# Attention's stores from SP to ACT, the order of two norms left free, and four embedding products ahead of the summed-weight products

## Chip, cores and metric

The kernel runs on one core of a Trainium2 chip. Times are device microseconds (us) of one execution; a time of the kernel is the median of its runs. The engines are named as in the profile: PE (TensorE, matmuls), DVE (VectorE), ACT (ScalarE), POOL (GpSimd), SP (SyncE, which here only issues DMA transfers). Each engine works through its own queue in order. SP and ACT can both issue transfers.

## What is computed

One layer of a decoder trunk for 1024 prompt tokens and 8 x 4 sample tokens, 1056 together, of width 1024. Cut to what matters:

```python
def _layer(x, p, attn_fn, pool_prev, pos0, ...):
    h = _rms(x, n_mix_pre)
    z = h @ w_in                      # q (8 heads x 64) | k, v (2 heads x 64) | pooling (4 x 128)
    a, k_state, v_state = attn_fn(q, k, v)            # window of 128 keys, a sink per head
    m, pool_state = _pool_mixer(u, pool_prev, pos0, w_pool, pool_scale)
    mix = jnp.concatenate([a, m], axis=-1) @ w_out
    x = x + _rms(mix, n_mix_post)
    f = _rms(x, n_ffn_pre)
    f = (jax.nn.silu(f @ w_gate) * (f @ w_up)) @ w_down
    x = x + _rms(f, n_ffn_post)
    x = x + jax.nn.sigmoid(x @ w_ple_gate) * (p @ w_ple)
    return x, k_state, v_state, pool_state
```

Besides y, the layer returns its states: the last 128 prompt keys and values, the last 15 pooling inputs, and the shifted key, value and pooling buffers of the samples. These states are the seven small stores of attention that the change moves.

## The kernel before

**Tiling.** Activations lie with the channels on 128 partitions and the tokens along the free axis. The 1056 tokens are cut into three groups (g = 0, 1, 2) of 352, so that a product is a chain of 128x128 by 128x352 matmuls into one PSUM bank. All float32 operands are split into a high and a low part (`split`, L164 on ACT for the high part, L165 on DVE for the low one), and a product takes three matmuls for each 128 channels: high x high, high x low, low x high (`gemm`, L126 is the line on which every matmul is recorded).

**Order.** The program is put in order by a scheduler that works on a simulated time: an instruction goes to its engine's queue when what it needs is ready there, and among ready ones the one that is written earlier goes first. The written order is therefore not the order of the queues, except where `tc.keep_in_program_order` pins an instruction behind everything written before it on its engine. `pinned[0]` pins the matmuls; `order(ins)` pins while `ordered[0]` is true; `load` pins on SP. Large working tiles share 28 slots (`act_tile`); a tile waits until a slot is free.

**Stages.** First come the three input norms and the pooling columns of w_in (`u_prod`, `u_evict`). A norm is `rstd_steps`: a matmul against ones sums the squares over the partitions, ACT takes the root (L323), DVE the reciprocal (L324) and its two parts (L326, L327), then `dg1` and `dg2` (L331, L337) write them on a diagonal, and a product spreads the diagonal over the partitions. The squares are added in `sum_halves` (L357, L358, L360), whose first addition is pinned through `order`. Then follow k, v and the four q products with the pooling mixer between them, and after them:

- L618 loads the prompt masks `am`. L628 to L636 transpose v; ACT copies the transposes to `vtok`, `vmix` and `vdec` (L630 to L636).
- L637 and L638 store the last keys and values (`kp_o`, `vp_o`); L603 and L604, earlier, store the pooling states (`pp_o`, `ps_o`).
- L757 to L759 load the cached keys `ckt`, the cached values `cvt` and the sample mask `dmt`.
- `dscores` multiplies the sample queries with the cached keys; L770 adds `dmt` to the scores on DVE, `softmax` follows (L659 to L673: maxima on DVE, exponentials on ACT at L667, scaling on POOL at L673). `scores(b)` does it for a block of 128 prompt queries (L706 and L707 put the two halves of the window together).
- `dturned` transposes the sample weights (L120) and copies them (L781, L782), `dvalues` multiplies with the values. Pieces of the output projection (`filler`) are written between these steps to keep PE at work.
- L863 to L865 store the shifted buffers `ks_o`, `vs_o`, `vn_o`; `kse` is put together for that on POOL.
- Then come the eight blocks of prompt queries, the rest of the fillers, and the loads of x for the residual (L880).

All these transfers are issued from SP before. The FFN fills the time from about 260 us to 1010 us.

**The end.** The last sub-layer multiplies x with w_ple_gate (`ple_out` for group 2, and for groups 0 and 1 a scheme with seven half-size products for four: `ple_first` and `ple_rest`). `ple_rest(a, b)` uses sums of two weight tiles, which `w_sums` makes: four additions on POOL (L1008, in place), then ACT and DVE split the two results (`sh`, `sl`). POOL's first addition has to wait until DVE has split half of the raw tile (`w`). It runs for the pairs (1,0), (3,2), (5,4), (7,6). `ple_end` takes the sigmoid (L1219), multiplies with the embedding product p @ w_ple (L1221), adds x (L1223) and stores a piece of y (L1224). The embedding product is six matmuls (`embed`); `embed_early` computes it ahead and keeps it in a tile, as all of group 0 has it:

```python
    for a in (7, 5, 3, 1):
        ple_first(a)
    finish(list(chains))
    for a, b in PAIRS:
        ple_rest(a, b)
```

Of the kernel before, what the change touches and what calls it, by code (L numbers as in the profile page):

```python
# [19 lines left out]
SEQ = 1024  # L20
NDEC, DSEQ = 8, 4
# [10 lines left out]
WIN = 128  # L32
NB = SEQ // WIN
# [28 lines left out]
def trunk_kernel(  # L62
# [31 lines left out]
    nc = tc.nc  # L94
    te, ve, se, ge = nc.tensor, nc.vector, nc.scalar, nc.gpsimd
# [14 lines left out]
    def act_tile(shape, dt=F32, s="a"):  # L110
        return apool.tile(shape, dt, tag="a", bufs=A_SLOTS, name=nm(s))

    def half(g, dt=F32, s="h"):
        return act_tile([P, 4, NS[g]], dt, s)
# [15 lines left out]
    def bank():  # L130
        return psum.tile([P, 512], F32, tag="b", name=nm("b"))

    def tmp(n, s="t", dt=F32):
        return spool.tile([P, n], dt, tag="tmp", bufs=6, name=nm(s), padded_shape=[P, NX])

    def const(shape, src=None, s="c", dt=F32):
        t = cpool.tile(shape, dt, name=nm(s))
        if src is not None:
            nc.scalar.dma_start(t, src)
        return t  # L140
# [17 lines left out]
    def fix(ins):  # L158

        if fixed[0]:  # L160
            tc.keep_in_program_order(ins)
# [76 lines left out]
    WPE = [[], []]  # L238
# [14 lines left out]
    W1 = {a: WPE[0][a] if a == KC - 1 else None for a, _ in PAIRS}  # L253
# [16 lines left out]
    def need(k, ahead=LOOK):  # L270

        for i in range(len(made), min(k + ahead + 1, len(ITEMS))):
            kind, js = ITEMS[i]
            if kind in ("direct", "home"):
                w_split(js[0], act_tile if kind == "home" else None)
                made[i] = pairs[js[0]]
            elif kind == "half":
                w_load(js[0])
                t = w_tile([P, KC, P], "w2")
                made[i] = t[:, 0:4, :], t[:, 4:8, :]  # L280
                split(*made[i], raws[js[0]][:, 4:8, :])
            else:
                for j in js:
                    w_load(j)
                made[i] = w_sums(*(raws[j] for j in js))
            for kind, js in ITEMS[i + 1 : i + 3]:
                for j in js:
                    w_load(j)
        return made[k]

    def gemm(ps, ops, start=True, stop=True):

        last = len(ops) - 1
        for i, (wh, wl, xh, xl) in enumerate(ops):
            mm(ps, wh, xh, start=start and i == 0, stop=False)
            mm(ps, wh, xl, start=False, stop=False)
            mm(ps, wl, xh, start=False, stop=stop and i == last)
# [9 lines left out]
    ordered = [True]  # L307
# [46 lines left out]
    def sum_halves(sqs, g):  # L354

        a, b = sqs
        order(ve.tensor_tensor(a, a, b, op=ALU.add))  # L357
        ve.tensor_tensor(a[:, 0:2, :], a[:, 0:2, :], a[:, 2:4, :], op=ALU.add)  # L358
        acc = acc_tile(g)
        ve.tensor_tensor(acc, a[:, 0, :], a[:, 1, :], op=ALU.add)  # L360
        return acc
# [37 lines left out]
    def x_squares(g):  # L399
        sqs = [xr[g, h] for h in range(2)]  # L400
        for t in sqs:
            fix(se.activation(t, t, AF.Square))
        acc1[g] = sum_halves(sqs, g)
# [57 lines left out]
    stt, pso = (sts[:, i * n : (i + 1) * n].rearrange("p (c b t) -> p c b t", c=4, t=PST) for i in range(2))  # L461
    pfx = sts[:, 2 * n : 2 * n + 64].rearrange("p (c t) -> p c t", c=4)
    ppo = sts[:, 2 * n + 64 :].rearrange("p (c t) -> p c t", c=4)
# [24 lines left out]
    def u_prod(c, g, h):  # L488

        if h == 0:  # L490
            ups[c, g] = bank()
        ps = ups[c, g][:, : NS[g]]
        wh, wl = pairs[U0[c]]
        xh, xl = xs[g][h]
        for k in range(4):
            mm(ps, wh[:, 4 * h + k, :], xh[:, k, :], start=h == 0 and k == 0, stop=False)
            mm(ps, wh[:, 4 * h + k, :], xl[:, k, :], start=False, stop=False)
        for k in range(4):
            mm(ps, wl[:, 4 * h + k, :], xh[:, k, :], start=False, stop=h == 1 and k == 3)

    def u_evict(c, g):
        for v, cols in toks(us[c], g):
            ve.tensor_tensor(v, like(ups[c, g][:, cols], v), like(r1[g][:, cols], v), op=ALU.mult)

    def u_norm(steps, g):
        try:
            next(steps)
        except StopIteration as e:
            se.copy(acc1[g], e.value)
            r1[g] = acc1[g]  # L510
# [9 lines left out]
    x_operand(2, 0, behind=True)  # L520
    u_norm(norms[0], 0)
    x_squares(1)
    for c in range(4):
        u_evict(c, 0)
        if c:
            u_prod(c, 1, 0)
# [21 lines left out]
    for c in (2, 3):  # L548
        for h in range(2):
            u_prod(c, 2, h)  # L550
        u_evict(c, 2)

    ordered[0] = False

    def u_pool(c):
        ue, dec = us[c], u_decode(c)
# [43 lines left out]
        if 1 <= i < 5:  # L600
            u_mix(i - 1)
    kT, vT, qT = qkv[0], qkv[1], qkv[2:]
    nc.sync.dma_start(pp_o, ppo)  # L603
    nc.sync.dma_start(ps_o, pso)  # L604
    pinned[0] = False


# [1 line left out]
    qd, am, vdec = misc[:, 0, :], misc[:, 1:5, :], misc[: NDEC * DSEQ, 5, :]  # L609
# [5 lines left out]
        own = qm[:, c * n : c * n + NDEC * QS].rearrange("p (b s) -> p b s", s=QS)  # L615
        ge.tensor_copy(own[:, :, :DSEQ], new.rearrange("p (b j) -> p b j", j=DSEQ))
    ys = [[half(g, s="y"), None] for g in range(G)]
    nc.sync.dma_start(am, masks)  # L618
    nskp, nskd = const([P, 8]), const([P, 2])
    ge.tensor_scalar(nskp, skp, -1.0, None, op0=ALU.mult)  # L620
    ge.tensor_scalar(nskd, skd, -1.0, None, op0=ALU.mult)
# [1 line left out]
    vtok, vmix = act_tile([P, NB, P]), act_tile([P, NB, P])  # L623
# [10 lines left out]
    ps = bank()  # L634
    te.transpose(ps[: NDEC * DSEQ, :P], vT[:, SEQ:], ident)
    se.copy(vdec, ps[: NDEC * DSEQ, :P])  # L636
    nc.sync.dma_start(kp_o, kT[:, SEQ - WIN : SEQ])  # L637
    nc.sync.dma_start(vp_o, vtok[:, NB - 1, :])  # L638

    def put(o, lo_tok, n):  # L640

# [112 lines left out]
    cvt = act_tile([P, NDEC, P])  # L754
# [89 lines left out]
    def filler(n):  # L844
        for _ in range(n):
            if fill:
                f, *at = fill.pop(0)
                f(*at)
# [11 lines left out]
    kse = act_tile([P, NDEC, WIN])  # L860
    ge.tensor_copy(kse[:, :, : WIN - DSEQ], ckt[:, :, DSEQ:])
    ge.tensor_copy(kse[:, :, WIN - DSEQ :], kT[:, SEQ:].rearrange("p (b t) -> p b t", t=DSEQ))
    nc.sync.dma_start(ks_o, kse)  # L863
    nc.sync.dma_start(vs_o, cvt[DSEQ:, :, :])
    nc.sync.dma_start(vn_o, vdec)  # L865
    for a, b in zip(blocks, blocks[1:] + [None]):
        t2 = None if b is None else scores(b)
        filler(1)
# [2 lines left out]
        values(a, parts)  # L871
        t = t2
    filler(len(fill))


    x1 = [[None] * 2 for _ in range(G)]
# [15 lines left out]
    def turn(n):  # L892

        now[0] += n
        for ch in [ch for ch in chains if ch[2]] or list(chains):
            while ch in chains and ch[1] <= now[0]:
                try:
                    load, wait = next(ch[0])
                except StopIteration:
                    chains.remove(ch)  # L900
                    break
                dve[0] = max(dve[0], now[0]) + load / share[0]
                ch[1] = dve[0] + wait
# [5 lines left out]
    def finish(ch_list):  # L909
        for ch in ch_list:  # L910
            for _ in ch[0]:
                pass
            chains.remove(ch)
# [107 lines left out]
    def quarter(w, h):  # L1021
        return tuple(t[:, 4 * h : 4 * h + 4, :] for t in w)
# [174 lines left out]
    def embed(wp, m, g):  # L1197

        ph, pl = pls[g]
        wh, wl = need(wp)  # L1200
        cols = slice((m % 4) * P, (m % 4 + 1) * P)
        pp = bank()
        gemm(pp[:, :N], [(wh[:, k, cols], wl[:, k, cols], ph[:, k, :], pl[:, k, :]) for k in range(2)])
        turn(6)
        return pp[:, :N]

    def embed_early(m, g, tiles=[None, None]):

        if m % 4 == 0:
            tiles[m // 4] = half(g, s="pp")  # L1210
        v = tiles[m // 4][:, m % 4, :]
        se.copy(v, embed(WPE[0][m][0], m, g))
        early[m, g] = v

    def ple_end(gate, wp, m, g):

        pp = early.pop((m, g)) if (m, g) in early else embed(wp, m, g)
        sg = tmp(N, "sg")
        se.activation(sg, gate, AF.Sigmoid)  # L1219
        xm = x2[g][m // 4][:, m % 4, :]  # L1220
        ve.tensor_tensor(sg, sg, pp, op=ALU.mult)  # L1221
        yo = tmp(N, "yo")
        ve.tensor_tensor(yo, sg, xm, op=ALU.add)  # L1223
        nc.sync.dma_start(y_o[:, m, OFF[g] : OFF[g + 1]], yo)  # L1224
# [9 lines left out]
    def product(w, x):  # L1234
        ps = bank()
        gemm(ps[:, :N], ops4(w, x))
        turn(12)
        return ps[:, :N]
# [3 lines left out]
    def ple_first(a):  # L1242

        wp, w = W1[a]
        need(wp)
        wg = need(w)
        if not p1s:
            p1s.append(half(0, s="p1"))
        p1 = p1s[0][:, a // 2, :]
        se.copy(p1, product(quarter(wg, 0), e7["B11"]))  # L1250
        c11 = tmp(N, "c11")
        ve.tensor_tensor(c11, p1, product(quarter(wg, 1), e7["B21"]), op=ALU.add)
        ple_end(c11, wp, a, 0)
# [32 lines left out]
        last_down(END, m, 1)  # L1286
    chain(ple_steps(1), 54)
    for m in range(FIRST):
        embed_early(m, 0)
    for m in range(FIRST, KC):  # L1290
        ple_out(m, 2)
        embed_early(m, 0)
    finish(chains[:1])
    for a in (7, 5, 3, 1):
        ple_first(a)
    finish(list(chains))
    for a, b in PAIRS:
        ple_rest(a, b)
# [86 lines left out]
```

## Time and profile before

| | |
|---|---|
| median of 3 runs | 1138.85 us (1133.57 to 1139.66) |
| profiled execution | 1138.72 us |
| span of its instructions | 1136.7 us |
| PE busy | 1111.0 us (98%) |
| DVE / ACT / POOL busy | 783.9 / 457.9 / 201.2 us |
| mean granted TensorE clock | 0.991 |

The profiled execution's own time is 2.0 us longer than its span: the rest lies before the first and behind the last instruction. PE is busy nearly all the time, so what is to be read is the list of places where PE isn't, and what ended each of these gaps. In a row of the timeline stand the start (us from the span's start), the duration (us; a merged row covers several instructions), the engine, the line, the operation, out<-in by tile names, the shapes and the count; in brackets stands how long the engine had been idle before it and what ended that. SPq and ACTq are the queues' DMA issues. In a row of the windows stand the stretch, its length, and for each engine the busy time and the number of instructions, then the granted TensorE clock, the share of the DMA engines' time and GB/s.

### The profile page before, as it was taken

What the parts mean: (1) busy time and instruction counts of PE and PEld (TensorE: products, weight loads), DVE (VectorE), ACT (ScalarE), POOL (GpSimd) and SP (SyncE); (2) the same over time, 40 slices, a digit from 0 to 9 for tenths busy, and PEclk for the clock granted to TensorE, in tenths of its full rate; (3) what the DMA queues carried; (4) which work ended last, traced back from release to release, by engine and by line L of the source; (5) the groups of instructions that cost most, each with busy time, mean ns of one, the idle gap of its engine ahead of it and who ended that gap; (6) DMA issues with size and microseconds to landing.
All of it is one profiled execution on the core that took longest, in us unless ns stands there. A gap on an engine that the chain in (4) does not pass through costs nothing.

```text
span 1136.7 us, 17509 instructions
## 1 busy us (share of the span) xinstructions
PE 1111.0 (98%) x6997; PEld 1091.9 (96%) x6997; DVE 783.9 (69%) x1296; ACT 457.9 (40%) x819; POOL 201.2 (18%) x169
## 2 busy tenths in 40 slices
PE   9999979999999999999999999999999999999987
PEld 8999967899999999999999999999999999999987
DVE  6666268975879955255464555548887877788887
ACT  8322257754646523331222313123524324356442
POOL 1044022200000131011111102111231132100241
PEclk9999989999999999999999999999999999999999
DMA  7121210362553212121110202113212212245241
GB/s 284 56 69 49 86 52 25 121 245 71 194 171 122 101 37 75 38 74 38 37 64 12 81 32 75 37 38 125 79 48 93 75 56 93 94 144 201 76 140 74
DMA packets 35985, 101.78 MB, mean 90 GB/s; under 512 B 4260, under 2 KB 14916, under 8 KB 35904
## 3 DMA queue, kind: packets, MB, share of 16 engines
q1 hardware_dynamic: 35616, 100.62, 26.1%
q8 instruction: 55, 0.90, 0.3%
q14 instruction: 26, 0.21, 0.1%
q10 hardware_dynamic: 288, 0.05, 0.0%
HBM read 90.55 MB, written 10.11 MB: 89 GB/s over the span
## 4 chain that ended last, share of the span: by engine, by line
PE 89%; DVE 5%; POOL 2%; issue 2%; ACT 1%; DMA 1%; POOLq 0%; SPq 0%; DVEq 0%; ACTq 0%
PE b L126 88%; POOL wr L1008 2%; PE b L120 1%; ACT sh L164 0%; DMA wr<-in_w_gu_dram 0%; DVE o L1131 0%; DVE wl L165 0%; DVE sg L1221 0%; DMA a<-in_dmask_dram 0%; DVE yo L1223 0%; ACT a L667 0%; DMA xr<-in_x_dram 0%; ACT wh L164 0%; DVE o L1150 0%; DVE x L1154 0%
## 5 line engine op out<-in xcount | busy, mean ns | idle before, releaser
L126 PE MATMUL b<-hid,wh 128*128 128x352 f32 x1056 | 254.7, 323 | 2.6 <-DVE o L1150 2.2
L164 ACT CAST wh<-wr 128x1024 fp32r<-128x1024 f32 (+1 forms) x135 | 138.6, 1029 | 254.0 <-PE b L126 203.3
L126 PE MATMUL b<-fh,wl 128*128 128x352 f32 x712 | 230.5, 324 | 0.0
L126 PE MATMUL b<-fh,wh 128*128 128x352 f32 x712 | 230.5, 324 | 0.0
L126 PE MATMUL b<-fl,wh 128*128 128x352 f32 x712 | 229.0, 322 | 0.0
L1008 POOL TENSOR_TENSOR wr<-wr 128x512 f32<-128x512 f32 x52 | 72.0, 1385 | 745.9 <-DVE wl L165 460.1
L165 DVE TENSOR_TENSOR wl<-wr,wh 128x1024 fp32r<-128x1024 f32 (+1 forms) x135 | 165.3, 1227 | 44.1 <-ACT wh L164 43.6
L126 PEld LDWEIGHTS b<-hid,wh 128*128 128x128 f32 x1056 | 185.1, 189 | 3.3 <-issue 2.4
L126 PE MATMUL b<-hid,wl 128*128 128x352 f32 x528 | 170.7, 323 | 0.0
L126 PE MATMUL b<-fh,sh 128*128 128x352 f32 x416 | 135.2, 325 | 2.9 <-ACT sh L164 1.9
L1105 DVE TENSOR_TENSOR o<-o,b 128x352 f32<-128x352 f32 x240 | 115.1, 515 | 31.7 <-PE b L126 31.5
L126 PE MATMUL b<-fh,sl 128*128 128x352 f32 x416 | 135.0, 325 | 0.7 <-DVE sl L165 0.7
L126 PEld LDWEIGHTS b<-fl,wh 128*128 128x128 f32 x712 | 135.3, 190 | 0.0
L126 PE MATMUL b<-fl,sh 128*128 128x352 f32 x416 | 134.2, 323 | 0.0
L126 PEld LDWEIGHTS b<-fh,wh 128*128 128x128 f32 x712 | 133.8, 188 | 0.0
L126 PEld LDWEIGHTS b<-fh,wl 128*128 128x128 f32 x712 | 133.7, 188 | 0.0
L165 DVE TENSOR_TENSOR sl<-wr,sh 128x1024 fp32r<-128x1024 f32 x52 | 63.6, 1222 | 81.5 <-ACT sh L164 81.3
L164 ACT CAST sh<-wr 128x1024 fp32r<-128x1024 f32 x52 | 54.0, 1048 | 146.4 <-POOL wr L1008 105.3
L126 PE MATMUL b<-h,wh 128*128 128x352 f32 x480 | 105.7, 326 | 1.3 <-ACT h L392 1.1
L126 PEld LDWEIGHTS b<-hid,wl 128*128 128x128 f32 x528 | 98.9, 187 | 0.0
L126 PEld LDWEIGHTS b<-h,wh 128*128 128x128 f32 x480 | 82.4, 190 | 2.3 <-ACT h L392 1.3
L126 PEld LDWEIGHTS b<-fh,sh 128*128 128x128 f32 x416 | 78.5, 189 | 3.4 <-ACT sh L164 2.2
(186 smaller groups left out, 1693.6 us busy)
## 6 DMA issues: line engine op xcount, KB each, us to landing
wr<-in_w_gu_dram SPq DMA_DIRECT2D x64, 512.0 KB, 3.2
wr<-in_w_dn_dram SPq DMA_DIRECT2D x32, 512.0 KB, 3.5
wr<-in_w_pg_dram SPq DMA_DIRECT2D x18, 512.0 KB, 3.3
x<-in_x_dram SPq DMA_DIRECT2D x6, 704.0 KB, 10.3
x1d<-x SPq DMA_DIRECT2D x6, 704.0 KB, 3.6
x<-x1d SPq DMA_DIRECT2D x6, 704.0 KB, 6.2
out_y_dram<-yo SPq DMA_DIRECT2D x24, 176.0 KB, 1.8
wr<-in_w_out_b_dram SPq DMA_DIRECT2D x8, 512.0 KB, 3.4
```

Source lines behind the costliest of these rows:

```text
L120: ins = te.transpose(out, src, ident)
L126: ins = te.matmul(*args, **kw)
L164: fix(se.copy(hi, src))
L165: fix(ve.tensor_tensor(lo, src, hi.bitcast(F32), op=ALU.subtract))
L1008: ge.tensor_tensor(out, a, b, op=op)
L1105: ve.tensor_tensor(o, o, v, op=ALU.add)
```

## The change

It has three parts.

1. The seven stores of the states (`pp_o`, `ps_o`, `kp_o`, `vp_o`, `ks_o`, `vs_o`, `vn_o`) are taken from SP; they are written behind the last `filler` and issued from ACT. The load of the prompt masks (`am`) is issued from ACT too, at its old place.
2. `ordered[0] = False` stands behind the squares of group 1 rather than behind the whole stage, so that `order` no longer pins the first addition of the squares of group 2 and the diagonals of groups 1 and 2.
3. `embed_early` gets the index of the weights as an argument, and four calls for group 1 (m = 0 to 3) stand between `ple_first` and `ple_rest`. `ple_end` then finds these four products in a tile of group 1 (a new tile of the 28 slots).

```diff
     x_squares(1)
+    ordered[0] = False
     for c in range(4):
         u_evict(c, 0)
...
-    ordered[0] = False
-
...
-    nc.sync.dma_start(pp_o, ppo)
-    nc.sync.dma_start(ps_o, pso)
...
-    nc.sync.dma_start(am, masks)
+    nc.scalar.dma_start(am, masks)
...
-    nc.sync.dma_start(kp_o, kT[:, SEQ - WIN : SEQ])
-    nc.sync.dma_start(vp_o, vtok[:, NB - 1, :])
...
-    nc.sync.dma_start(ks_o, kse)
-    nc.sync.dma_start(vs_o, cvt[DSEQ:, :, :])
-    nc.sync.dma_start(vn_o, vdec)
...
     filler(len(fill))
+    nc.scalar.dma_start(pp_o, ppo)
+    nc.scalar.dma_start(ps_o, pso)
+    nc.scalar.dma_start(kp_o, kT[:, SEQ - WIN : SEQ])
+    nc.scalar.dma_start(vp_o, vtok[:, NB - 1, :])
+    nc.scalar.dma_start(ks_o, kse)
+    nc.scalar.dma_start(vs_o, cvt[DSEQ:, :, :])
+    nc.scalar.dma_start(vn_o, vdec)
...
-    def embed_early(m, g, tiles=[None, None]):
+    def embed_early(wp, m, g, tiles=[None, None]):
 
         if m % 4 == 0:
             tiles[m // 4] = half(g, s="pp")
         v = tiles[m // 4][:, m % 4, :]
-        se.copy(v, embed(WPE[0][m][0], m, g))
+        se.copy(v, embed(wp, m, g))
         early[m, g] = v
...
     for m in range(FIRST):
-        embed_early(m, 0)
+        embed_early(WPE[0][m][0], m, 0)
     for m in range(FIRST, KC):
         ple_out(m, 2)
-        embed_early(m, 0)
+        embed_early(WPE[0][m][0], m, 0)
     finish(chains[:1])
     for a in (7, 5, 3, 1):
         ple_first(a)
+    for m in range(4):
+        embed_early(W1[1][0], m, 1)
     finish(list(chains))
```

## The prediction

> **What bounds the kernel now.** I read the page's busy times first, then stretches around each place where PE pauses, then queue by queue what ended the pause.
>
> ```profile
> span 1136.7 us, 17509 instructions
> PE 1111.0 (98%) x6997; PEld 1091.9 (96%) x6997; DVE 783.9 (69%) x1296; ACT 457.9 (40%) x819; POOL 201.2 (18%) x169
> ```
>
> PE pauses for some 25 us in all, and nothing else can be won without fewer matmuls. The change touches three of the pauses. The largest lies at the start of attention (windows; after the engines' busy times comes the granted clock):
>
> ```profile
> 142.70:145.67 2.97, 0.01 (x2) 0.00 (x1) 1.97 (x9) 2.37 (x10) 0.72 (x1) 1.00 0.35 106
> 145.67:148.24 2.57, 2.57 (x16) 2.26 (x16) 1.96 (x8) 0.98 (x7) 0.00 (x0) 1.00 0.24 77
> 148.24:151.45 3.21, 0.00 (x1) 0.03 (x1) 1.22 (x6) 3.16 (x16) 1.04 (x1) 0.91 0.15 57
> 151.45:157.70 6.25, 6.25 (x53) 4.72 (x53) 1.06 (x3) 0.91 (x3) 2.14 (x3) 0.50 0.21 85
> ...
> 153.90:157.70 3.80, 3.80 (x19) 2.63 (x17) 1.06 (x3) 0.91 (x3) 0.00 (x0) 0.50 0.34 138
> 164.16:166.10 1.94, 1.94 (x21) 1.48 (x17) 1.37 (x6) 1.29 (x4) 1.09 (x2) 1.00 0.00 0
> ...
> DVE a L770 <- DMA a<-in_dmask_dram: 6.2, 1, 6.2
> ```
>
> PE stands for 2.97 and 3.21 us, together 6.18, with 2.57 us of filler between, and then runs 6.25 us at half the clock. The list of waits (last row) has DVE waiting 6.2 us for the sample mask. Why that comes late stands in SP's queue:
>
> ```profile
> 71.05 0.33 SPq L637 DMA_DIRECT2D out_kp_dram<-a  x1
> ...
> 123.44 0.39 SPq L618 DMA_DIRECT2D a<-in_masks_dram  x1
> 123.98 0.33 SPq L757 DMA_DIRECT2D a<-in_ck_dram  x1
> 136.75 0.34 SPq L638 DMA_DIRECT2D out_vp_dram<-a  x1
> 137.15 0.42 SPq L758 DMA_DIRECT2D a<-in_cv_dram  x1
> 137.63 2.07 SPq L759 DMA_DIRECT2D a<-in_dmask_dram  x1
> ```
>
> Between 124.3 and 136.75 SP issues nothing. The next in its queue is the store of the last values; it needs `vtok`, which ACT copies (below) until 136.7. The loads of `cvt` and `dmt` stand behind it. The mask lands about 142.0, and the softmax of the samples starts there.
>
> **Part 1, attention's transfers.** Eight issues leave SP (0.33 to 0.39 us each), and with `vp_o` the wait that holds up two loads. How early `dmt` can start: its slot comes free at the latest when the last projection product is done (133.5, where the transposes of L628 begin).
>
> ```profile
> 16.70 0.34 ACTq L464 DMA_DIRECT2D a<-in_pfix_dram  x1
> ...
> 133.48 1.04 PE L628 MATMUL b<-c,a 128*128 128x128 f32 x8
> ...
> 136.57 1.04 PE L126 MATMUL b<-a,a 64*128 64x32 f32 x10
> ...
> 136.14 0.58 ACT L630 COPY a<-b 128x512 f32<-128x512 f32 x1
> ...
> 137.71 0.25 ACT L636 COPY a<-b 32x128 f32<-32x128 f32 x1
> ...
> 142.00 0.56 DVE L770 TENSOR_TENSOR a<-b,a 128x160 f32<-128x160 f32 x2 [6.17 <-DMA a<-in_dmask_dram]
> ...
> 143.30 0.43 ACT L667 ACTIVATE a<-a,nmx 128x160 f32<-128x160 f32 x1 [5.34 <-DVE nmx L661]
> ...
> 150.90 0.41 DVE L782 COPY a<-b 32x256 f32<-32x256 f32 x1
> ```
>
> Latest: issued at 133.5 plus 0.8 for two issues, landed 4.4 later (137.63 to 142.0), 138.7; a gain of 3.3. Earliest: the scores of L770 are ready when the first matmuls of the row at 136.57 are, about 137.1; a gain of 4.9. ACT needs its first exponential 1.3 after L770, at 138.4, but copies until 137.96 and may then issue two or three stores (0.34 each, by the ACTq row): up to 0.6 later. I take 4.6. From L770 to the end of L782 (142.00 to 151.31) everything hangs together on DVE, ACT and POOL, so `dvalues` starts at 151.45 - 4.6 = 146.85. PE, with 2.57 of filler straight behind 142.70, is free at 145.3: a pause of 1.6 in place of 6.2. PE is then full to the end of attention, so the 4.6 stays.
>
> The clock is the second half. A pause within 142.70:145.67 left it at 1.00; the next halved it for 6.25 us. Eight score products took 3.80 us at half clock (153.90:157.70) and 1.94 for the same work at full (164.16:166.10): 1.85 lost; the remaining 2.45 us are `dvalues`, of which half, 1.2, could be lost, and I take half of that. So 2.5 (bounds 0 and 3.1) if 1.6 us of pause don't halve the clock. What halves it is to be seen at one more place:
>
> ```profile
> 1015.27:1017.37 2.10, 0.00 (x0) 0.00 (x0) 2.10 (x8) 1.52 (x3) 0.00 (x0) 1.00 0.63 228
> 1017.87:1021.28 3.41, 3.41 (x14) 3.41 (x13) 3.41 (x6) 0.95 (x2) 0.00 (x0) 0.50 0.00 0
> ```
>
> A pause of 2.10 did it; 2.97 at 142.70 didn't at once. 1.6 is shorter than both, so I expect full clock, but not by much. The Trainium skill ("TensorE: Matmul & The Clock Gate", Part 1, What's actually happening) puts the half clock behind a whole idle window of about 3.4 us that runs free of the kernel; by it 1.6 us costs nothing and the sum stays at 1128.8, by the row of 2.10 us the clock could still fall and the sum be 1131.3; the trace disagrees with a whole idle window, since 2.10 was enough.
>
> Where the stores go: the row at 71.05 shows that the queue doesn't keep the written order. `kp_o` is written behind the transposes of v, which run at 133.48, and was issued 62 us before them, when the keys were there. So I expect the stores in ACT's queue at about their old times, each 0.34 us, 2.7 with the masks if all of it fell on the path; spread over 100 us of an engine that is busy 457.9 of 1136.7 us, I count only the 0.3 in the 4.6. The masks move to ACT at about 123 and are used behind L770 (142.00): cost nothing, 18 us of cover. The waits of `pp_o` (on POOL) and `vs_o` (on the load of `cvt`) now stand in ACT's queue, with exponentials and weight splits behind them; if a store comes up there before its data, these wait, and PE behind them.
>
> **Part 2, the norms.** The diagonals depend on the instruction before them, so the pin costs them nothing. The addition of group 2's squares is another matter:
>
> ```profile
> 34.79 1.38 ACT L402 ACTIVATE xr<-xr 128x1408 f32<-128x1408 f32 x1 [3.76 <-DVE h L393]
> ...
> 41.38 0.18 DVE L324 RECIPROCAL sd<-sd 128x3 f32<-128x3 f32 x1 [6.02 <-ACT sd L323]
> ...
> 42.87 1.62 DVE L357 TENSOR_TENSOR xr<-xr,xr 128x1408 f32<-128x1408 f32 x1
> ...
> 46.03 0.83 PE L126 MATMUL b<-c,acc 128*128 128x1 f32 x6 [0.70 <-DVE acc L360]
> ```
>
> Its squares are there at 36.2 and DVE is idle until 41.38, yet it runs behind the diagonals of group 1, and PE waits 0.70 us. Unpinned it takes 36.2 to 39.3 of DVE's idle time: 0.7 won, at most that, at least nothing. If it came up in the queue late, it and its two followers (42.87 to 46.03, 3.1 us) would push the diagonals; the 6 us of idle time are the cover.
>
> **Part 3, the end.** Four groups of six matmuls move. From 1089.50 to the next product is 0.95, so 3.8 in all, to where PE waits for the sums of pair (1,0):
>
> ```profile
> 1079.20:1081.20 2.00, 0.06 (x2) 0.04 (x1) 0.05 (x1) 1.13 (x2) 0.83 (x1) 1.00 0.00 0
> 1081.20:1087.80 6.60, 5.93 (x26) 5.64 (x27) 6.57 (x9) 2.27 (x4) 2.24 (x2) 0.74 0.55 168
> ...
> 1089.50 1.12 PE L126 MATMUL b<-pl,a 128*128 128x352 f32 x6
> 1090.45 0.32 PE L126 MATMUL b<-fh,sh 128*128 128x352 f32 x1
> ...
> 1044.47 0.45 ACT L1212 COPY pp<-b 128x352 f32<-128x352 f32 x1 [0.96 <-PE b L126]
> ...
> 1080.07 1.04 ACT L164 CAST sh<-wr 128x1024 fp32r<-128x1024 f32 x1 [4.21 <-POOL wr L1008]
> ...
> 1104.95 1.22 DVE L165 TENSOR_TENSOR sl<-wr,sh 128x1024 fp32r<-128x1024 f32 x1 [2.26 <-ACT sh L164]
> ...
> 1107.87 0.32 PE L126 MATMUL b<-fh,sh 128*128 128x352 f32 x1
> ...
> 1117.41 1.23 PE L126 MATMUL b<-pl,a 128*128 128x352 f32 x6 [0.79 <-DVE sg L1221]
> ```
>
> Upper bound 3.8. It isn't all won, since the sums come from a chain that doesn't hurry: POOL, ACT (`sh`), DVE (`sl`), for each pair again. Late next is pair (5,4): its `sl` ends at 1106.17; PE, which took its first product with them at 1107.87 and needs `sl` two matmuls on (1108.2), can start 2.0 earlier and no more. Behind that PE is full but for 0.79 at 1117.41, which goes too, since the product whose reader ended that wait is now ahead: 2.8. Against it stand four more copies on ACT, 0.45 each (row of L1212); they fall due from 1078 to 1081.5, and one or two stand before `sh` at 1080.07 and shift the whole chain, by 0 to 1.6; I take 0.7. Left 2.1 (bounds 0.4 and 3.8). The clock of 0.74 behind the pause rises, but there DVE sets the pace (6.57 of 6.60 us).
>
> **Sum.** 0.7 + 4.6 + 2.5 + 2.1 = 9.9 us less than the profiled execution's 1138.72 (span 1136.7 and 2.0 around it; 0.13 under the median of 1138.85): 1128.8.
>
> **Rivals.** *Half clock all the same:* the 1.6 us of pause halve it, 1131.3. For it the 2.10 at 1015; against it 2.97 at 142.70.
>
> *The end gives nothing:* copies and a new order of DVE take it back, 1130.9. For it DVE's 6.57 of 6.60 us; against it its idle time before 1104.95.
>
> *Another queue saves only the time of the issue:* the mask is late for another reason, as its 2.07 us at issue might say, five times the 0.42 of the load before it. Then part 1 gives 0, since 8 x 0.34 on an idle SP shortens nothing: 1138.7 - 0.7 - 2.1 = 1135.9. The Trainium skill ("DMA: Bandwidth & Descriptors", Issuing engines are not separate DMA queues) says that issuing from several engines saves only the sequencer's time. Against it stand the 12.4 us in which SP waited with two loads queued.
>
> *Slower:* ACT is blocked. If the stores do stand behind the last block, they come at about 220, together with the six loads of x and ACT's last split whose product PE needs next (230.37):
>
> ```profile
> 230.37 1.05 ACT L164 CAST wh<-wr 128x1024 fp32r<-128x1024 f32 x1 [3.22 <-PE b L126]
> ...
> x<-in_x_dram SPq DMA_DIRECT2D x6, 704.0 KB, 10.3
> ```
>
> Seven stores are 2.4 us, and a wait behind one such load 10.3: 12.7 against 9.9, 1141.5. It decides once ACT stands for more than 9.9 us. Against it the row at 71.05.
>
> **Chances.** As summed 0.45; half clock 0.20; nothing at the end 0.15; only the issue 0.13; ACT blocked 0.07. 0.5%, about what a measurement here can tell from no change, is 5.7 us. The first three are faster by more (0.80, less 0.05 for sums that fall short together); the fourth and most of the fifth lie within: faster 0.75, same 0.21, slower 0.04. All upper bounds together give 0.7 + 4.9 + 3.1 + 3.8 = 12.5, 1126.2; I set the low end at 1125.0, and the high one at 1136.5, just past "only the issue".
>
> **What would show it.** Right: the mask is issued by 134, L770 starts within a us of the scores, and the pauses between there and `dvalues` fall to 1 to 2 us at a clock of 1.00; L357 of group 2 runs before the reciprocal of group 1; PE has work from 1077 to 1081 (less the shift), and its gaps at 1096 and 1117 shrink. Wrong: `dmt` waits for something but the store; an ACT row stands behind a store with several us of idle time; the `sh` casts come later than POOL.

## The result, and the profile after

The changed kernel takes 1130.5 us (median of 8 runs, 1129.6 to 1131.3), the kernel before 1136.6 (8 runs, 1132.9 to 1139.7): a ratio of 0.9946, 95% interval 0.9928 to 0.9963. That is 6.1 us, where 9.9 were forecast from the profiled execution of 1138.72, which lay 2.1 over the median of all 8 runs. The page of the changed kernel begins:

```profile
span 1128.6 us, 17518 instructions
PE 1105.4 (98%) x6997; PEld 1085.6 (96%) x6997; DVE 785.1 (70%) x1296; ACT 459.3 (41%) x823; POOL 200.7 (18%) x169
```

**Start of attention.** Windows of the changed kernel (after the engines' busy times: granted clock, DMA share, GB/s):

```profile
144.80:146.90 2.10, 0.00 (x0) 0.03 (x1) 1.02 (x5) 2.05 (x10) 1.04 (x1) 1.00 0.15 59
...
148.64:152.05 3.41, 3.41 (x17) 2.36 (x14) 1.06 (x3) 0.92 (x4) 0.48 (x2) 0.50 0.37 154
```

One pause of 2.10 us stands where two of 6.18 together stood, and the clock is halved for 3.41 us, not 6.8. Its timeline shows why, on SP's and ACT's queues and the instructions that end the chain:

```profile
125.62 0.33 SPq L754 DMA_DIRECT2D a<-in_dmask_dram  x1
...
60.43 0.36 ACTq L866 DMA_DIRECT2D out_pp_dram<-a  x1
...
136.49 0.34 ACTq L869 DMA_DIRECT2D out_vp_dram<-a  x1
137.73 0.34 ACTq L872 DMA_DIRECT2D out_vn_dram<-a  x1
138.16 0.53 ACTq L871 DMA_DIRECT2D out_vs_dram<-a  x1
138.74 0.43 ACT L662 ACTIVATE a<-a,nmx 128x160 f32<-128x160 f32 x1 [1.05 <-DVE es L658]
...
136.64 0.56 DVE L765 TENSOR_TENSOR a<-b,a 128x160 f32<-128x160 f32 x2 [1.09 <-PE b L126]
...
146.90 4.91 PE L126 MATMUL b<-a,a 32*64 32x128 f32 x52 [2.10 <-ACT y L802]
```

The mask is issued at 125.62 (137.63 before). The mask's addition now waits for the scores (PE), no longer for a DMA, and starts 5.36 us earlier (142.00 to 136.64); `dvalues` starts 4.55 earlier (151.45 to 146.90). The missing 0.8 is ACT's: the three stores stand between 136.5 and 138.7, and the first exponential follows the addition by 2.10 us, 1.30 before. The stores, written behind the last block, are issued at about their old times; none of them comes behind it.

**Norms.** L357 of group 2 runs at 36.48 (42.87 before); PE's wait of 0.70 at 46 is gone, and 0.21 us stand at the next norm (50.32).

**The end.** What PE waited for from 1050 us on (total, times, longest), first the kernel before, then the changed one:

```profile
PE b L126 <- ACT sh L164: 1.9, 1, 1.9
PE b L126 <- DVE p L1260: 1.0, 1, 1.0
PE b L126 <- DVE sg L1221: 0.8, 1, 0.8
PE b L126 <- DVE sl L165: 0.7, 1, 0.7
```

```profile
PE b L126 <- DVE sl L165: 4.8, 5, 1.8
PE b L126 <- DVE p L1259: 0.5, 1, 0.5
```

4.4 us before, 5.3 after. The pause before pair (1,0) is filled, and the same time stands again in five waits for the low halves `sl` of the later pairs. The first addition of the weight sums of pair (1,0) on POOL, and those of (5,4) and (7,6), in the kernel before and then the changed one:

```profile
1073.38 1.30 POOL L1008 TENSOR_TENSOR wr<-wr 128x512 f32<-128x512 f32 x1 [92.12 <-DVE w L165]
...
1097.74 1.29 POOL L1008 TENSOR_TENSOR wr<-wr 128x512 f32<-128x512 f32 x1 [6.09 <-DVE w L165]
...
1108.85 1.28 POOL L1008 TENSOR_TENSOR wr<-wr 128x512 f32<-128x512 f32 x1 [5.02 <-DVE w L165]
```

```profile
1064.38 1.30 POOL L1007 TENSOR_TENSOR wr<-wr 128x512 f32<-128x512 f32 x1 [90.11 <-DVE w L165]
...
1088.58 1.30 POOL L1007 TENSOR_TENSOR wr<-wr 128x512 f32<-128x512 f32 x1 [5.89 <-DVE w L165]
...
1101.48 1.51 POOL L1007 TENSOR_TENSOR wr<-wr 128x512 f32<-128x512 f32 x1 [7.02 <-DVE w L165]
```

The sums keep their own pace: (5,4) starts 24.4 us after (1,0) before and 24.2 after, although PE is ahead of them by a pause; (7,6) follows 11.1 us later before and 12.9 after. From the first of these additions to the end of the span it is 1136.7 - 1073.38 = 63.32 before and 1128.6 - 1064.38 = 64.22 after: at the end the change *loses* 0.90.

Between these places two stretches differ that no part of the change touches. PE's pauses at 879 and 1017 us of the kernel before, and the same two of the changed one:

```profile
879.03 0.56 PE L126 MATMUL b<-hid,wh 128*128 128x352 f32 x2 [2.15 <-DVE o L1150]
...
1017.37 0.59 PE L126 MATMUL b<-dg,c 128*128 128x352 f32 x2 [2.10 <-DVE dg L337]
```

```profile
873.38 0.56 PE L126 MATMUL b<-hid,wh 128*128 128x352 f32 x2 [2.11 <-DVE o L1149]
...
1009.92 0.58 PE L126 MATMUL b<-dg,c 128*128 128x352 f32 x2 [2.10 <-DVE dg L337]
```

The gain is 5.65 at the first and 7.45 at the second, so 1.8 came in 140 us of the same products, at a granted clock of 1.00. From the one pause to the other it is 136.5 us in ten of the fourteen profiled kernels, 137.4 in two (e3 and e10 below) and 138.3 in two (the kernel before and e4, which has parts 1 and 2), so the length goes with no part of the change. The pause of 2.10 then halved the clock in the one execution (the row of 1017.87 in the prediction) and not in the other:

```profile
1010.50:1014.00 3.50, 3.50 (x24) 3.50 (x23) 3.50 (x6) 0.95 (x2) 0.00 (x0) 1.00 0.00 0
```

At POOL's first addition the gain is 9.00, 1.55 more. These 3.35 us, of the 8.1 by which the two spans differ, are differences between two executions. What is the change's is 4.55 at `dvalues` (mask and norms together), 1.1 more by 879, and -0.90 at the end: 4.75.

### The profile page after: what moved, and what is told of

Its sections match the earlier page's. It is cut to its first block, busy times and chain, and to the rows that moved or that the text cites. A ratio compares the mean times of both kernels' runs of the same rounds, so it can differ in the third digit from the quotient of the medians.

```text
span 1128.6 us, 17518 instructions
## 1 busy us (share of the span) xinstructions
PE 1105.4 (98%) x6997; PEld 1085.6 (96%) x6997; DVE 785.1 (70%) x1296; ACT 459.3 (41%) x823; POOL 200.7 (18%) x169
## 4 chain that ended last, share of the span: by engine, by line
PE 87%; DVE 4%; ACT 3%; issue 2%; POOL 1%; DMA 1%; POOLq 0%; ACTq 0%; SPq 0%; DVEq 0%
PE b L126 87%; POOL wr L1007 1%; DMA xr<-in_x_dram 1%; PE b L120 1%; ACT h L392 1%; ACT wh L164 0%; DVE sg L1220 0%; DVE yo L1222 0%; DVE o L1130 0%; ACT sh L164 0%; ACT a L662 0%; DMA c<-in_gains_dram 0%; DVE o L1149 0%; DMA wr<-in_w_in_dram 0%; DVE x L1153 0%
## 5 line engine op out<-in xcount | busy, mean ns | idle before, releaser
L126 PEld LDWEIGHTS b<-fh,sl 128*128 128x128 f32 x416 | 77.9, 187 | 6.3 <-DVE sl L165 6.3
```

The source lines that it names most:

```text
L126: ins = te.matmul(*args, **kw)
```

## The experiments

Each was timed in turns with the kernel before. The theory: the wait of one store in SP's queue is all that the change takes away; the norms are worth nothing to speak of, and the end is bound by the chain of the weight sums over POOL, ACT and DVE. Its rivals: the prediction's own sum, in which the end gives 2.1, and a second queue that helps by itself.

**The three parts alone.** e1_part1 holds only the hunks on the transfers, e2_part2 only those on `ordered[0]`, e3_part3 only those on `embed_early`; e4_no_end is the changed kernel without the last.

> Part 1 alone: the seven stores and the masks on ACT's queue, norms and end as before. Theory (the mask's wait in SP's queue is what the change took away): dvalues starts 4 to 5 us earlier, one stretch of half clock of 3.4 us in place of 6.8, together 5 to 6 us under the kernel before (ratio 0.995). Rival 1 (the sum of the prediction): 7.1 under (0.994). Rival 2 (another queue saves only the time of the issue, and the gain came from the other parts): 0 to 0.5.

> Part 2 alone: only the first norm keeps its order. Theory: the addition of group 2's squares goes into DVE's idle time at 36, PE's wait of 0.70 us at 46 goes, a new one of 0.2 us comes behind it: 0.3 to 0.7 us under the kernel before, within what a measurement can tell from nothing. Rival: the addition comes up late in DVE's queue and pushes the diagonals, 1 to 3 us over.

> Part 3 alone: four embedding products of group 1 ahead of the summed-weight products. Theory (the sums' chain over POOL, ACT and DVE sets the end, and DVE's new order lengthens it): 0 to 1 us over the kernel before; PE's waits of 1079 are gone and stand again at the later pairs. Rival (the prediction): 2.1 under; PE reaches the last product 2 us earlier.

> Parts 1 and 2 without part 3. Theory: as fast as the changed kernel or up to 1 us faster, 6 to 7 us under the kernel before (0.994 to 0.995). Rival (the prediction's 2.1 for the end): 2 us slower than the changed kernel, 4 under the kernel before (0.9965).

| kernel | median, us | ratio to before | 95% interval |
|---|---|---|---|
| part 1 | 1130.6 | 0.9944 | 0.9923 to 0.9964 |
| part 2 | 1136.3 | 0.9998 | 0.9983 to 1.0012 |
| part 3 | 1136.0 | 0.9998 | 0.9983 to 1.0013 |
| parts 1 and 2 | 1131.3 | 0.9949 | 0.9930 to 0.9969 |

Part 1 alone is the whole gain, as far as these times can tell. Parts 1 and 2 lie 0.8 over the changed kernel, where the theory had 0 to 1 under, but the intervals overlap. Parts 2 and 3 alone show no gain; the interval of part 3 (1.9 us faster to 1.5 slower) just excludes the 2.1. Its trace is sharper than its time. What PE waited for from 1050 us on, and the first sum of pair (1,0), with part 3 alone:

```profile
PE b L126 <- DVE sl L165: 4.1, 5, 1.8
...
1072.80 1.30 POOL L1008 TENSOR_TENSOR wr<-wr 128x512 f32<-128x512 f32 x1 [91.87 <-DVE w L165]
```

To the end of its span (1137.0) it is 64.20 us. The eight profiled kernels that have the old end and the sums on POOL lie between 63.32 and 63.45, the three with part 3 between 64.20 and 64.29. So part 3 costs 0.8 to 0.9, an amount that the whole time doesn't resolve.

**Which of the eight transfers.** e5_vp_act changes one word, e6_others_act moves all but that one, and e7_order moves nothing to another queue:

```diff
e5  -    nc.sync.dma_start(vp_o, vtok[:, NB - 1, :])
    +    nc.scalar.dma_start(vp_o, vtok[:, NB - 1, :])
e7  -    nc.sync.dma_start(vp_o, vtok[:, NB - 1, :])
...
    -    nc.sync.dma_start(cvt, cv)
    -    nc.sync.dma_start(dmt, dmask)
    +    tc.keep_in_program_order(nc.sync.dma_start(cvt, cv))
    +    tc.keep_in_program_order(nc.sync.dma_start(dmt, dmask))
    +    tc.keep_in_program_order(nc.sync.dma_start(vp_o, vtok[:, NB - 1, :]))
```

> Of the whole change only one word: the store of the last values, vp_o, goes out on ACT; the other six stores and the masks stay on SP. Theory (that store's wait for vtok held the loads of cvt and dmt in SP's queue, and nothing else in part 1 matters): the mask is issued at about 125, dvalues starts 4 to 5 us earlier, 5 to 6 us under the kernel before (ratio 0.995), as part 1 alone. Rival 1 (SP is relieved by eight issues, each of 0.33 to 0.42 us): an eighth of that, under 1 us. Rival 2 (the mask is late for a reason of its own): 0.

> The complement: the other six stores and the masks go out on ACT, vp_o stays on SP where it was. Theory: the mask still waits behind vp_o, issued at about 137; the pauses before dvalues stay 6 us together and the time that of the kernel before within 0.1% (ratio 1.000). Rival 1 (SP is relieved): most of 6 us, 0.996 or less.

> No transfer changes its queue: on SP the loads of cvt and dmt are only put ahead of the store vp_o, and kept in that order. Theory (the order in one queue is what counts, not the queue): 5 to 6 us under the kernel before (0.995), as part 1 alone. Rival (the second queue itself is what helps, by transfers side by side or by ACT's issue): 0 to 2 us under.

Measured: e5 1128.45 (ratio 0.9940, 0.9924 to 0.9955), e6 1136.45 (1.0006, 0.9994 to 1.0018), e7 1128.45 (0.9939, 0.9924 to 0.9955). One store is the whole of part 1, and the queue it goes to doesn't matter. SP's queue in e6, then in e7:

```profile
136.58 0.35 SPq L636 DMA_DIRECT2D out_vp_dram<-a  x1
136.98 0.42 SPq L756 DMA_DIRECT2D a<-in_cv_dram  x1
137.50 1.74 SPq L757 DMA_DIRECT2D a<-in_dmask_dram  x1
```

```profile
126.05 0.33 SPq L758 DMA_DIRECT2D a<-in_dmask_dram  x1
136.92 0.34 SPq L759 DMA_DIRECT2D out_vp_dram<-a  x1
```

The store is issued at about the same time in both, when its data are there; only what stands behind it differs. e5 and e7 also leave ACT free of `vn_o` and `vs_o`. In e7 the mask's addition comes at 137.07, the first exponential 1.31 later, and the pause is 1.31, not 2.10:

```profile
138.38 0.43 ACT L666 ACTIVATE a<-a,nmx 128x160 f32<-128x160 f32 x1 [0.25 <-DVE nmx L660]
...
146.54 3.40 PE L126 MATMUL b<-a,a 32*64 32x128 f32 x52 [1.31 <-ACT y L807]
```

The medians of e5 and e7 lie 2.05 under the changed kernel's, but 1.5 of that is in the kernel before of the same rounds too (1135.0 beside 1136.6), and the intervals of the ratios overlap.

**Stores that really stand behind the last block.** e8_pinned is the changed kernel with each of the seven in `tc.keep_in_program_order(...)`.

> The changed kernel with its seven stores kept in their written order, so that ACT really issues them behind the last block, all seven in a row ahead of ACT's last sum of squares. Theory (stores whose data are long there cost ACT only the time of issue, 7 x 0.34 = 2.4 us, and PE has filler behind them): 0 to 2.4 us over the changed kernel, 1130.5 to 1133. The rival of the prediction (ACT is blocked behind them, 12.7 us of standing): 1141 or more.

Measured 1141.6 (1.0056, 1.0037 to 1.0075), eleven over the changed kernel: the theory's 0 to 2.4 fell, and the rival's time was met. ACT's queue and ACT behind it, two waits of PE, and the window behind the longer one:

```profile
228.36 0.35 ACTq L866 DMA_DIRECT2D out_pp_dram<-a  x1
...
232.92 0.52 ACTq L871 DMA_DIRECT2D out_vs_dram<-a  x1
235.96 0.33 ACTq L872 DMA_DIRECT2D out_vn_dram<-a  x1
236.33 0.50 ACT L808 ACTIVATE acc<-y 128x352 f32<-128x352 f32 x1 [6.28 <-DVE y L821]
...
PE b L126 <- DVE dg L337: 4.3, 1, 4.3
PE b L126 <- DVE a L720: 2.1, 3, 0.8
...
240.00:243.00 3.00, 2.94 (x10) 2.94 (x11) 2.39 (x4) 0.61 (x2) 0.00 (x0) 0.50 0.23 94
```

The seven issues, whose data had long been there, last from 228.4 to 236.3, and for the final 6.28 us ACT does nothing else: three take 0.5 to 1.2 us, and 1.3 and 2.5 us lie idle between the last ones, while the DMA engines are full (231 to 235: a share of 1.05). The loads of x are over by about 231 (the last is issued at 224.8, and none takes more than 6.4 us to land); what is under way then are the stores themselves and a load of weights issued at 230.0. The root of the norm stands behind them, PE waits 4.3 us, and the clock is halved after it. Another 4.5 us were lost between 188 and 205, before any of the seven (the product at 188.52 is 0.8 ahead of the changed kernel's, the one at 205.44 is 3.7 behind it): PE waits three times for L720, 2.1 us together, and the store of `kse` now keeps its slot of the attention tiles to the end. That this slot is the cause is argued, not shown.

**The weight sums.** e9_sums_dve has e7's order, part 3, and the sums of the last four pairs on DVE; e10_sums_dve_no_p3 is the same without part 3.

```diff
-                made[i] = w_sums(*(raws[j] for j in js))
+                made[i] = w_sums(*(raws[j] for j in js), ve if i > W2[1][1] else ge)
...
-            ge.tensor_tensor(out, a, b, op=op)
+            eng.tensor_tensor(out, a, b, op=op)
```

> The order of SP's queue (as in the run before), plus part 3, plus the weight sums of the last four pairs on DVE in place of POOL (four additions of 128x512: 0.68 each by the split of that shape on DVE, against 6 to 7 us on POOL). Theory (at the end PE waits for the chain POOL, ACT, DVE of the sums, 12 us per pair, so that part 3 only moved the wait): with 4 us taken out of each pass the chain no longer sets the pace and part 3 gives what the prediction had for it, 2 to 3.8 us: from the last norm's product to the end about 110 in place of 112.7 without part 3 and 113.5 with it; the time 1125 to 1126.5. Rival 1 (DVE itself is the bound there): DVE has 11 us more to do and the end grows by 1 to 4 us. Rival 2 (the ACT copies and the order of the queues cost the 0.8): no change against part 3 alone.

> The same without part 3: SP's order, and the last sums on DVE. Theory: the sums of pair (1,0) come 4 us earlier, so the pause of 1.94 before them and the one of 0.95 at pair (5,4) go: 2 to 3 us under the kernel with SP's order alone, the end 110 too; part 3 is then worth nothing, since PE doesn't wait. Rival (DVE is the bound): 0 to 3 us over.

Measured: e9 1122.4 (0.9890, 0.9875 to 0.9906), e10 1122.9 (0.9890, 0.9875 to 0.9905), both about 6 us under e7, twice what was expected. Eight of the sixteen additions in the kernel before (POOL) and in e10 (DVE), and what PE still waits for in e10:

```profile
L1008 POOL TENSOR_TENSOR wr<-wr,wr 128x512 f32<-128x512 f32 x8 | 12.4, 1554 | 0.6
...
L1008 DVE TENSOR_TENSOR wr<-wr,wr 128x512 f32<-128x512 f32 x8 | 5.5, 682 | 0.0
...
PE b L126 <- DVE sl L165: 0.7, 1, 0.7
PE b L126 <- DVE p L1260: 0.6, 1, 0.6
PE b L126 <- ACT sh L164: 0.2, 1, 0.2
```

PE's waits fall from 4.4 to 1.5 us, the pause of 1.9 us that halved the clock is gone, and the last result follows PE's last product sooner (1115.9 against 1114.7 in e10, 1123.6 against 1120.1 in e7). The rival fell: DVE was free enough. With the sums early, part 3 is worth nothing that these times show: the pause ahead of pair (1,0), which it was to fill, is down to the 0.2 us for `sh`. So the sums' chain did set the end.

**Filler in the pause.** e11_filler: e7 with `filler(2)` for `filler(1)` between `dturned` and `dvalues`.

> SP's order, and two products of filler in place of one before dvalues (one less at the end of attention). Theory (the pause of 1.3 us before dvalues is the wait left, and what can halve the clock there): PE has work in it, the pause goes, no half clock at 148 to 154 in any run; 1 to 3 us under the kernel with SP's order alone, 1126 to 1127.5. Rival (the filler is wanted at the end of attention, and dvalues and all that follows are late by it): 0 to 1 us over.

Measured 1130.8 (0.9960, 0.9948 to 0.9973), 2.3 over e7, more than the rival allowed. The pause and the half clock are gone, as expected, but `dvalues` starts at 147.15, 0.6 late, and PE waits at two of the later blocks for their transposed weights (L723), where it doesn't in e7 (the only other wait from 140 to 245 is 0.2):

```profile
PE b L126 <- DVE a L723: 0.8, 2, 0.4
```

The rest of the 2.3 isn't found in these rows.

**Together.** e12_best: e10 with part 2.

> What the runs so far point to, together: SP's order, the last sums on DVE, and part 2 (the first norm only keeps its order); all stores on SP, no product moved. Theory (part 2 takes away PE's wait of 0.70 us at 46 and puts one of 0.2 in its place, whatever is done behind it): 0.3 to 0.6 us under the kernel without part 2, about 1122.3, ratio 0.9885. Rival (the 0.5 is lost again at the next wait, as the runs with part 2 alone would allow): 0, about 1122.9.

Measured 1121.5 (0.9860, 0.9840 to 0.9880): 15.4 under its runs of the kernel before and 9 under the changed kernel, the lowest median here. Between e10 and e12 the medians differ by 1.4, but the intervals overlap.

## Why the prediction was right, and where not

Faster was right, and so was the main reason, the wait of the mask. Of the 9.9 us that were forecast (0.9%) 6.1 came (0.5%), and of the four terms one held in full. Point by point:

**The mask, 4.6 (3.3 to 4.9): right.** `dvalues` moved 4.55, which holds what the norms give as well; with part 1 alone it moved 4.42 (151.45 to 147.03), and 4.91 in e5 and e7, the upper bound, since there no store delays ACT's exponential. The 0.3 counted for ACT's stores was 0.5 to 0.8. e6 and e7 exclude the rival "only the time of the issue": one store's place in the queue is worth everything, the other seven transfers nothing.

**The half clock, 2.5 (0 to 3.1): the step that failed is "1.6 is shorter than both, so I expect full clock".** The length of a pause doesn't decide. Windows of 146 to 158 us in parts 1 and 2, in e5, and in e7:

```profile
146.00:158.00 12.00, 11.30 (x84) 9.69 (x84) 5.82 (x19) 4.83 (x21) 2.15 (x3) 0.72 0.12 50
...
146.00:158.00 12.00, 11.46 (x102) 9.25 (x102) 6.99 (x21) 6.11 (x27) 3.18 (x4) 0.86 0.15 62
...
146.00:158.00 12.00, 11.46 (x114) 9.54 (x116) 7.93 (x25) 7.26 (x31) 4.22 (x5) 1.00 0.15 60
```

A mean of 0.72 over 12 us is 6.7 us at half clock, 0.86 is 3.4, 1.00 none. The pauses ahead were 2.04, 1.25 and 1.31. Of the six kernels with a pause of 1.25 to 1.31 four had 3.4 us at half clock and two none; the three with 2.04 to 2.10 had 3.4, 3.4 and 6.7. The pause before the last norm (the row of 1015.27 in the prediction), 2.10 to 2.13 us in all fourteen profiled kernels, halved the clock in seven of them and not in the other seven. So these traces show a lottery and no better odds for a short pause, and an expected value would have been the right term. The changed kernel's profiled execution got 1.1 of the 2.5 by 879. The Trainium skill ("TensorE: Matmul & The Clock Gate", Part 1, What's actually happening) has the window of 3.4 us running free of the kernel, and the stretches of 3.41 agree; the halving after less than a whole idle window disagrees.

**The norms, 0.7 (0 to 0.7): within bounds.** The wait of 0.70 went and 0.21 came. `dvalues` comes 0.1 to 0.7 earlier in the traces with part 2 than in those without it (151.45 to 150.80 with part 2 alone, 146.41 to 145.96 from e10 to e12, 147.03 to 146.90 from e1 to the changed kernel); the time of part 2 alone doesn't tell it from nothing.

**The end, 2.1 (0.4 to 3.8): wrong in sign, -0.9.** The shift by ACT's copies, for which 0.7 was counted, didn't come: `sh` was cast as soon as POOL was done, and the copies came behind it. The step that failed is "can start 2.0 earlier": it took the times of the later sums as fixed and as early enough. They were fixed, but PE reached them sooner and waited, and DVE and ACT got another order. In it the half split `w` of pair (7,6), which POOL's sums need, stands behind a sigmoid that waits 2.79 us for an addition on DVE (ACT, the kernel before and then the changed one):

```profile
1106.16 0.61 ACT L164 CAST w<-wr 128x512 fp32r<-128x512 f32 x1
1109.79 0.50 ACT L1219 ACTIVATE sg<-c 128x352 f32<-128x352 f32 x1 [3.02 <-DVE c L1260]
```

```profile
1099.67 0.50 ACT L1218 ACTIVATE sg<-c 128x352 f32<-128x352 f32 x1 [2.79 <-DVE c L1259]
1100.08 0.60 ACT L164 CAST w<-wr 128x512 fp32r<-128x512 f32 x1
```

That agrees with the 1.8 us by which the sums of (7,6) follow later; the order alone wasn't tried. "There DVE sets the pace" isn't borne out either: e10 gave DVE 11 us more over the end, and the end got shorter.

**The sum.** Put with what the traces show, it is 4.55 for the mask and the norms together, 1.1 for the clock and -0.9 for the end, 4.75 us in place of 9.9, beside a measured 6.1 (4.2 to 8.2). Two of the rivals happened: the half clock came in part, and the end gave nothing. That 1128.8 still lies within 1.7 us of 1130.5 is partly luck: the sum was taken from an execution that lay 2.1 over the median of the kernel before. Taken from that median, 1136.6, it gives 1126.7, which is 3.8 too low.

**The rival "ACT is blocked"** was told apart by the row at 71.05: the queue doesn't keep the written order. Where it was made to (e8), the rival's 1141.5 was met by 1141.6, by other amounts than it had summed. Beside the kernel before that is luck too: e8 is 6.6 over its own runs of it (1135.0), where the rival stood 2.8 over (1138.7 to 1141.5).

## What to carry to other kernels

A queue's order is a chain of waits: look for the instruction at which an idle queue stands and ask what is behind it; one store put behind two loads gave all that eight moved transfers gave. Work moved into a pause is worth only what the next wait allows: measure the step from one of its releasers to the next (here 12 us a pair on POOL) and shorten that first. Where the clock can fall after a pause, put an expected value into the sum; take the sum from the median of several runs, not from the one that was profiled; and see whether a gain in one pair of traces lies at the places that the change touches.

## What was not expected of the hardware

Equal pauses halve PE's clock in one execution and not in another (1.25 and 1.30 us did, 1.30 and 1.31 didn't; 2.10 at 1017 did, and at 1009.92 after the change didn't), where it did for about 3.4 us or twice that. The same products over 140 us, at a granted clock of 1.00, took 136.5, 137.4 or 138.3 us by the execution; the cause is open. Issues of DMAs whose data are ready aren't always 0.34 us: seven in a row took 8 us while the DMA engines were full. And an addition of 128x512 took 0.68 us on DVE and 1.55 on POOL, so that the idler engine was the slower place.
